# A hybrid layer on one core: the preparation of the scan shifted by a few empty steps, and the split values stored in full rows

## The chip, the core and the metric

The kernel runs on one core of a Trainium2 chip. The metric is the time that the device takes for one execution, in microseconds (us). A core has five engines that matter here, each with a queue of its own, worked in order: TensorE (PE in the profile, its weight loads PEld), VectorE (DVE), ScalarE (ACT), GpSimd (POOL) and SyncE (SP, which issues most DMA transfers). Matmul results go to PSUM banks, everything else lies in SBUF or in HBM.

## What is computed

One layer over 1024 latent tokens (with 256 context tokens ahead of them, 1280 rows in all) of width 1024. Its input projection has two groups of columns: a gated DeltaNet (4 heads of 128, scanned in both directions in chunks) and a neighbourhood attention (8 heads of 64). Both are concatenated and projected back; a SwiGLU feed-forward follows. The parts that matter here:

```
px = modulate(rms_norm(x, norm1_w[i]), sh1, sc1) @ w_in[i]       # q k v z a b | nq nk nv
qkv = short_conv(p[..., :3 * DN_WIDTH], conv_w)                    # centred, 5 taps, then SiLU
decay = exp(where(tril, gam[..., :, None] - gam[..., None, :], -inf))
m = where(strict, einsum("bhncd,bhnmd->bhncm", kb, k) * decay, 0)
u = triangular_solve(eye + m, v * beta[..., None])                 # and w, with the same matrix
...
s_win = einsum("bnqhd,binchd->bhnqic", q_r, k_r) + bias            # windows of 8 rows x 32 columns
o = einsum("bhnqic,binchd->bnqhd", p_win, v_r) + einsum("bhnqk,bkhd->bnqhd", p[..., n_win:], v_ctx)
...
x = x + g1 * (concatenate([dn_x, na_x], -1) @ w_out[i])
x = x + g2 * swiglu(modulate(rms_norm(x, norm2_w[i]), sh2, sc2), w_ffn_in[i], w_ffn_out[i])
```

The inverses of the triangular matrices `eye + m` (chunks of 128 rows here, 10 per direction) are needed by the scan.

## The kernel before

**Jobs.** The input projection is a list of jobs, worked one after the other (the loop in the code below). A `Block` makes 128 columns for all rows, transposed: 8 steps over the contraction, each with three matmuls (high and low halves of a value: high by high, low by high, high by low; `mm_part`, L404) for each of two or three column pieces. A `Wide` makes 256 columns with rows on the partitions, one tile of 128 rows after the other (L592), and each tile reads the whole of its weights `zw`. The order is k0 to k3, z (second half), nk0 to nk2, nv (first half), nk3, q0 to q3, nq0 to nq3, v0, nv (second half), v1, v2, v3, z (first half, called z0 in the prediction). Then come the scan and the attention, the output projection and the feed-forward.

**Weights.** A weight tile is loaded into `wraw`, of which there is one buffer. ScalarE casts its high part (`whi` L198, for a Wide `zw` L584), GpSimd computes the low part (`wlo` L199, `zw` L585). A Wide has two such halves, so its second load waits until GpSimd is done with the first. These loads stand in SyncE's queue.

**Behind a Block.** ScalarE copies its PSUM pieces into `cr` (L452), VectorE applies the five taps (L456, L460), ScalarE the SiLU (L467).

**Background work.** Two generators are advanced by a step at a time while the jobs run: one step for each of a Block's 8 steps, 2 or 3 for each tile of a Wide. A `yield` is the end of a step. The generators set where an instruction is traced; a scheduler then decides each engine's order, unless an instruction is pinned with `keep_in_program_order`, which puts it behind all that its engine was given earlier.

- `block_inverses` makes the inverses of the 32 by 32 diagonal blocks. VectorE works on `N` in a loop (L880, L882), the diagonal is set (L885), and after four empty steps TensorE transposes it in groups of four (L892) into PSUM banks `m`, which ScalarE copies out (L894). Results go to `x_d` in HBM.
- `preps` builds the full inverses, chunk by chunk in both directions, ten preparations in all, at most two of them alive at once. For a preparation GpSimd builds `rg` (L952), TensorE sums it into decays (L964, L965), ScalarE takes the exponential, VectorE scales the block `kk` (L971), TensorE multiplies by `fx` (L984), ScalarE copies the scaled block back into `kk` (L987), and three merges follow (TensorE L995, copies on VectorE L997 and on ScalarE L998), each in a step of its own. The results go to `y_d` and `at_d` in HBM (L1007). Between the sums and the products lie two steps, behind the copy one. Matmuls here use two banks called `pr`.

**The split values.** `nv` is stored to `nv_d` by rows. After each half, SyncE issues copies from there into `vw_d` (L1104), which holds the values by column block and row group as the windows of the attention need them. The attention reads them as `vw` (L277).

Of the kernel before, what the change touches and what calls it, by code (L numbers as in the profile page):

```python
# [88 lines left out]
def hybrid(ctx, tc, a, dbg):  # L89
# [56 lines left out]
    nv_d = dram.tile([T, 512], F32, name="nv_d", tag="nv_d")  # L146
    nq_d = dram.tile([NAH, 2, ND, L], F16, name="nq_d", tag="nq_d")
    nk_d = dram.tile([2, NAH, ND, T], F16, name="nk_d", tag="nk_d")
    vw_d = dram.tile([128, 4, 4, 4, 128], F32, name="vw_d", tag="vw_d")
    y_d = dram.tile([2, NCH, 128, 4, 128], F32, name="y_d", tag="y_d")  # L150
    at_d = dram.tile([2, 8, 128, 4, 128], F32, name="at_d", tag="at_d")
    x_d = dram.tile([128, 2, 2, NU, 32], F32, name="x_d", tag="x_d")
# [100 lines left out]
    def attention(nw):  # L253
# [20 lines left out]

        def values(hp, half, cb):
            vw = nw.tile([128, 3, 128], F32, name="vw", tag="vw", bufs=3)
            sp.dma_start(vw, vw_d[:, hp, cb, half:half + 3])  # L277
            return vw

        def context(hp):  # L280
# [93 lines left out]
    with ExitStack() as bs:  # L374
# [445 lines left out]
        def block_inverses():  # L820
            with ExitStack() as gs:
# [61 lines left out]
                    yield  # L883
                flat = N.rearrange("p b r c -> p b (r c)")
                dve.memset(flat[:P, :, 0:1024:33], 1.0)  # L885
                for _ in range(4):
                    yield
                U = WK.rearrange("p d u i -> p (d u) i")
                for i0 in range(0, 32, 4):
                    p = bank()  # L890
                    for i in range(4):
                        pe.transpose(p[:, i * P:(i + 1) * P], N[:P, :, :, i0 + i].rearrange("p b r -> p (b r)"),  # L892
                                     ident[:P, :P])
                    act.copy(U[:, :, i0:i0 + 4], p[:, :4 * P].rearrange("p (i u) -> p u i", i=4))  # L894
                    if i0 % 8 == 4:
                        yield
# [15 lines left out]
        def preps():  # L912

            first_half.close()
            with ExitStack() as gs:
                pk = pools(gs, "pk", "left")
                shift(gs, "ppad", "left", 64)
                pp = pools(gs, "pp", "left")

                def work(name, bufs=2, dt=F32):  # L920
                    return (pk if name == "kk" else pp).tile([128, 4, 128], dt, name=name, tag=name, bufs=bufs)

                fxs = [work(f"fx{d}", 1) for d in range(2)]
                ys = [[work(f"y{d}{i}", 1) for d in range(2)] for i in range(2)]
                for t in fxs + ys[0] + ys[1]:
                    pool.memset(t, 0.0)
                q32 = [slice(b * 32, b * 32 + 32) for b in range(4)]

                def fetch(i):

                    got = []
                    for d in range(2):
                        c = ORDER[d][i]
                        kk, xc = work("kk", 6), pp.tile([128, 2, 4, 32], F32, name="xc", tag="xc", bufs=4)
                        sp.dma_start(kk, kk_d[:, c])
                        sp.dma_start(xc, x_d[:, d, :, c * 4:c * 4 + 4])
                        at = None
                        if c >= 2:
                            at = work("at", 4)
                            sp.dma_start(at, qk_d[:, c - 2])  # L940
                        got.append((d, c, kk, xc, at))
                    return i, got

                def prep(i, got):
                    y = ys[i % 2]
                    rgs = []
                    for d, c, kk, xc, at in got:
                        mle = M[C_LE + d].rearrange("p (o i) -> p o i", o=1).to_broadcast([128, 4, 128])
                        for gg in (GH, GL):
                            rg = work("rg", 4, F32R)  # L950
                            g = gg.bitcast(F32)[:, d, c].rearrange("p (h o) -> p h o", o=1).to_broadcast([128, 4, 128])
                            pool.tensor_tensor(rg, g, mle, OP.mult)  # L952
                            rgs.append(rg)
                    for d, c, kk, xc, at in got:
                        for q in q32:
                            act.copy(fxs[d][q, :, q], xc[q, 1])
                    yield 1
                    if i == 0:
                        yield 1
                    es = []  # L960
                    for d, c, kk, xc, at in got:
                        p = bank("pr")
                        for j in range(2):
                            pe.matmul(p, mr[:, d], fl(rgs[2 * d + j]), start=j == 0, stop=False)  # L964
                        pe.matmul(p, mr[:, 4], mneg[:, d].rearrange("p (o i) -> p o i", o=1).to_broadcast(  # L965
                            [128, 4, 128]), start=False, stop=True)
                        e = work("e", 2)
                        act.activation(fl(e), p, AF.Exp)
                        es.append(e)
                    for (d, c, kk, xc, at), e in zip(got, es):  # L970
                        dve.tensor_tensor(kk, kk, e, OP.mult)  # L971
                    for (d, c, kk, xc, at), e in zip(got, es):
                        for q in q32:
                            pool.tensor_copy(y[d][q, :, q], xc[q, 0])
                        if at is not None:
                            dve.tensor_tensor(at, at, e, OP.mult)
                            stores.append((at_d[d, c - 2], at, tick[0] + 2))
                    yield 1
                    yield 1
                    ps = []  # L980
                    for d, c, kk, xc, at in got:
                        p = bank("pr")
                        for h in range(4):
                            pe.matmul(p[:, hs[h]], kk[:, h], fxs[d][:, h], start=True, stop=True)  # L984
                        ps.append(p)
                    for (d, c, kk, xc, at), p in zip(got, ps):
                        act.copy(fl(kk), p)  # L987
                    yield 1
                    for n in range(1, 4):
                        blk = (q32[3 - n], q32[n])  # L990
                        cols = (slice(128 - 32 * n, 128), slice(0, 32 * n))
                        ps = [bank("pr").rearrange("p (h i) -> p h i", h=4) for _ in got]
                        for h in range(4):
                            for (d, c, kk, xc, at), p in zip(got, ps):
                                pe.matmul(p[blk[d], h, :32 * n], kk[:, h, blk[d]], y[d][:, h, cols[d]],  # L995
                                          start=True, stop=True)
                        dve.tensor_copy(y[0][blk[0], :, cols[0]], ps[0][blk[0], :, :32 * n])  # L997
                        act.copy(y[1][blk[1], :, cols[1]], ps[1][blk[1], :, :32 * n])  # L998
                        yield 1
                    for d, c, kk, xc, at in got:  # L1000
                        stores.append((y_d[d, c], y[d], tick[0] + 1))

                stores, tick = [], [0]

                def flush(n):
                    while stores and stores[0][2] <= n:
                        sp.dma_start(*stores.pop(0)[:2])  # L1007

                todo = list(range(NCH))
                live, landing = [], []  # L1010
                while live or todo or landing:
                    if not landing and todo and (todo[0] < 2 or all(x in done for x in queries)):
                        landing.append(fetch(todo.pop(0)))
                    if landing and (not live or len(live) < 2 and live[0][1] >= 4):
                        live.append([prep(*landing.pop(0)), 0])
                    if not live:
                        yield
                    for g in list(live):
                        tick[0] += 1
                        flush(tick[0])  # L1020
                        g[1] += 1
                        if not next(g[0], 0):
                            live.remove(g)
                        yield
                flush(tick[0] + 2)
# [23 lines left out]
        for n in range(2, len(jobs) + 2):  # L1049
# [44 lines left out]
            for _ in fin:  # L1094
                pass
            done.add(n - 2)
            if isinstance(j, Wide) and j.kind == "nv":
                hv = slice(2 * j.half, 2 * j.half + 2)
                vlat = nv_d[CT:].rearrange("(r c) d -> r c d", c=64)
                for cb in range(4):  # L1100
                    for ch in range(4):
                        for r in range(4):
                            rows = vlat[4 * ch + r, BLKS[cb]:BLKS[cb] + 32].rearrange("c (h d) -> c h d", d=128)
                            sp.dma_start(vw_d[r * 32:r * 32 + 32, hv, cb, ch], rows[:, hv])  # L1104
            if nrm:
                nrm.norm()
            if isinstance(j, Block):
# [665 lines left out]
```

## Time and profile before

| | |
|---|---|
| median of 3 runs | 1541.6 us (1541.44 to 1543.45) |
| the profiled execution | 1541.49 us |
| its span on the core | 1539.4 us |
| mean granted clock of TensorE | 0.988 |
| busy: TensorE, VectorE, ScalarE, GpSimd | 1474.1, 993.6, 728.2, 234.8 us |
| `vw_d` stores: number, size, median landing | 128, 32.0 KB, 2.2 us |
| `vw` loads: number, size, median landing | 32, 192.0 KB, 3.8 us |

TensorE is busy for 96% of the span. What is left is a list of short waits, which the profile names by the waiting tile and line and by the instruction that ended the wait. The granted clock is the share of its full rate that TensorE was given. The edited stages lie between about 250 and 580 us of the span.

### The profile page before, as it was taken

To read this page: it belongs to the slowest core of one execution; us is meant where nothing else is said; L and a number is where in the kernel's file an instruction comes from. 1 tells how busy PE (TensorE), PEld (TensorE's weight loads), DVE (VectorE), ACT (ScalarE), POOL (GpSimd) and SP (SyncE) were. 2 spreads that over 40 slices of the span, in tenths; PEclk is the share of its full clock that TensorE was granted. 3 is DMA by queue.
4 is the path that set the end of the run, shared out by engine and by line. 5 is a ranking of instruction groups with operands and counts; after the bars stand their busy time and mean duration, and the time that the engine had idled before them with its cause. 6 is when DMAs were issued, how large, how long until landed. Compare 5 with 4: busy or idle time off the path is not lost. (4 is left out here: it accounts for less than half of the span.)

```text
span 1539.4 us, 24029 instructions
## 1 busy us (share of the span) xinstructions
PE 1474.1 (96%) x8702; PEld 1231.0 (80%) x8702; DVE 993.6 (65%) x1712; ACT 728.2 (47%) x1405; POOL 234.8 (15%) x286
## 2 busy tenths in 40 slices
PE   6999998899899898999999999999999999999999
PEld 3788797777688787788888878888888888888887
DVE  4774587974464354677977379855555566599652
ACT  5442552646764236666873176333333334354440
POOL 1054500634554100111210000000000000000000
PEclk9999999999999999999999999999999999999999
DMA  9274232687655557898638503533333334798742
GB/s 387 68 212 139 60 86 79 202 239 246 182 172 170 147 142 247 278 292 253 209 90 282 183 34 109 186 106 106 107 105 103 104 102 148 248 376 275 247 143 82
DMA packets 205142, 267.36 MB, mean 174 GB/s; under 512 B 17760, under 2 KB 115552, under 8 KB 204000
## 3 DMA queue, kind: packets, MB, share of 16 engines
q1 hardware_dynamic: 194320, 258.45, 52.4%
q10 hardware_dynamic: 10704, 7.38, 1.5%
q8 instruction: 68, 1.11, 0.3%
q14 instruction: 50, 0.41, 0.1%
HBM read 201.02 MB, written 68.94 MB: 175 GB/s over the span
## 5 line engine op out<-in xcount | busy, mean ns | idle before, releaser
L404 PE MATMUL blk<-hh,whi 128*128 128x512 f32 (+1 forms) x410 | 123.0, 394 | 6.8 <-ACT cr L452 5.3
L1410 ACT CAST uhi<-ws 128x512 fp32r<-128x512 f32 x91 | 54.0, 621 | 146.0 <-PE ps L1349 96.1
L1410 ACT CAST uhi<-wq 128x512 fp32r<-128x512 f32 x101 | 61.0, 622 | 130.9 <-issue 84.6
L404 PE MATMUL blk<-hl,whi 128*128 128x512 f32 (+1 forms) x410 | 115.4, 375 | 0.3 <-DVE hl L704 0.3
L404 PE MATMUL blk<-hh,wlo 128*128 128x512 f32 (+1 forms) x410 | 114.6, 375 | 0.6 <-POOL wlo L199 0.6
L592 PE MATMUL blk<-zw,hh 128*128 128x256 f32 (+1 forms) x576 | 113.5, 291 | 1.1 <-ACT cr L452 1.0
L1411 DVE TENSOR_TENSOR ulo<-wq,uhi 128x512 fp32r<-128x512 f32 x101 | 67.5, 687 | 58.4 <-ACT uhi L1410 32.4
L1349 PE MATMUL ps<-hT,uhi 128*128 128x512 f32 x336 | 103.6, 390 | 0.0
L1349 PE MATMUL ps<-lT,uhi 128*128 128x512 f32 x336 | 103.5, 389 | 0.0
L1349 PE MATMUL ps<-hT,ulo 128*128 128x512 f32 x336 | 103.4, 389 | 0.0
L592 PEld LDWEIGHTS blk<-zw,hh 128*128 128x128 f32 x576 | 91.7, 191 | 4.0 <-ACT cr L452 1.5
L1349 PE MATMUL ps<-hB,uhi 128*128 128x512 f32 x288 | 89.2, 391 | 0.6 <-ACT hB L1524 0.6
L1349 PE MATMUL ps<-lB,uhi 128*128 128x512 f32 x288 | 88.8, 389 | 0.4 <-DVE lB L1525 0.4
L1349 PE MATMUL ps<-hB,ulo 128*128 128x512 f32 x288 | 88.6, 389 | 0.0
L404 PEld LDWEIGHTS blk<-hh,whi 128*128 128x128 f32 x410 | 69.0, 194 | 21.9 <-ACT cr L452 6.1
L404 PEld LDWEIGHTS blk<-hl,whi 128*128 128x128 f32 x410 | 72.5, 192 | 14.9 <-DVE hl L704 0.8
L404 PEld LDWEIGHTS blk<-hh,wlo 128*128 128x128 f32 x410 | 72.5, 192 | 14.9 <-POOL wlo L199 0.9
L592 PE MATMUL blk<-zw,hl 128*128 128x256 f32 (+1 forms) x288 | 82.4, 286 | 0.0
L199 POOL TENSOR_TENSOR wlo<-wraw,whi 128x1024 fp32r<-128x1024 f32 x18 | 46.6, 2586 | 194.1 <-ACT whi L198 193.9
L1349 PEld LDWEIGHTS ps<-lT,uhi 128*128 128x128 f32 x336 | 63.1, 188 | 13.2
L1349 PEld LDWEIGHTS ps<-hT,ulo 128*128 128x128 f32 x336 | 63.1, 188 | 13.2
L1349 PEld LDWEIGHTS ps<-hT,uhi 128*128 128x128 f32 x336 | 62.9, 188 | 12.9
(362 smaller groups left out, 3526.1 us busy)
## 6 DMA issues: line engine op xcount, KB each, us to landing
wq<-w_fo SPq DMA_DIRECT2D x99, 256.0 KB, 4.1
wq<-w_gu SPq DMA_DIRECT2D x88, 256.0 KB, 2.9
wad<-wa SPq DMA_DIRECT2D x64, 256.0 KB, 4.2
bt<-rpb SPq DMA_DIRECT2D x64, 192.0 KB, 3.7
t_d<-g SPq DMA_DIRECT2D x22, 512.0 KB, 3.7
fr<-t_d SPq DMA_DIRECT2D x44, 256.0 KB, 5.2
f_d<-g SPq DMA_DIRECT2D x33, 256.0 KB, 2.1
fr<-f_d SPq DMA_DIRECT2D x33, 256.0 KB, 4.2
```

Source lines behind the costliest of these rows:

```text
L199: lo_engine.tensor_tensor(o, r, h.bitcast(F32), OP.subtract)
L404: pe.matmul(o, ww[:, k], xx[k][:, s], start=k == 0 and j == 0, stop=k == KT - 1 and j == 2)
L592: pe.matmul(p[:, :c1 - c0], x[k][:, s], ww[:, k, c0:c1], start=k == 0 and j == 0, stop=k == KT - 1 and j == 2)
L1349: pe.matmul(o, w[wi][:, k], x[xi][:, k], start=first and k == 0 and j == 0, stop=k == n - 1 and j == 2, skip_group_check=True)
L1410: act.copy(hi, self.raw[key])
L1411: dve.tensor_tensor(lo, self.raw[key], hi.bitcast(F32), OP.subtract)
```

## The change

Four edits. The transposes of the inverse come after six empty steps instead of four, and the first of each group is pinned to its place in program order. The first sums of preparation 0 come ten steps behind its `rg` instead of two (`LATE`; the ordinary step stays), and are pinned; the count that lets preparation 1 start begins lower by as much. Each preparation has one more empty step between the copy of the scaled block and the first merge. And `vw_d` holds full rows of 512 values: instead of 64 stores of 32 KB after each half of nv there are 16 stores of 256 KB after the second half, and a read of `vw` picks 128 of the 512 values in each of its three rows.

```
-    vw_d = dram.tile([128, 4, 4, 4, 128], F32, name="vw_d", tag="vw_d")
+    vw_d = dram.tile([128, 4, 4, 512], F32, name="vw_d", tag="vw_d")
...
-            sp.dma_start(vw, vw_d[:, hp, cb, half:half + 3])
+            sp.dma_start(vw, vw_d[:, cb, half:half + 3, hp * 128:hp * 128 + 128])
...
-                for _ in range(4):
+                for _ in range(6):
                     yield
...
-                        pe.transpose(p[:, i * P:(i + 1) * P], N[:P, :, :, i0 + i].rearrange("p b r -> p (b r)"),
-                                     ident[:P, :P])
+                        t = pe.transpose(p[:, i * P:(i + 1) * P], N[:P, :, :, i0 + i].rearrange("p b r -> p (b r)"),
+                                         ident[:P, :P])
+                        if not i:
+                            tc.keep_in_program_order(t)
...
                     yield 1
-                    if i == 0:
+                    for _ in range(LATE if i == 0 else 0):
                         yield 1
...
-                            pe.matmul(p, mr[:, d], fl(rgs[2 * d + j]), start=j == 0, stop=False)
+                            m = pe.matmul(p, mr[:, d], fl(rgs[2 * d + j]), start=j == 0, stop=False)
+                            if i == 0:
+                                tc.keep_in_program_order(m)
...
                         act.copy(fl(kk), p)
                     yield 1
+                    yield 1
...
-                stores, tick = [], [0]
+                LATE, stores, tick = 10, [], [0]
...
-                        live.append([prep(*landing.pop(0)), 0])
+                        live.append([prep(*landing.pop(0)), 0 if live or len(todo) < NCH - 1 else -LATE])
...
-            if isinstance(j, Wide) and j.kind == "nv":
-                hv = slice(2 * j.half, 2 * j.half + 2)
-                vlat = nv_d[CT:].rearrange("(r c) d -> r c d", c=64)
+            if isinstance(j, Wide) and n == values:
+                vlat = nv_d[CT:].rearrange("(n r c) d -> r c n d", r=4, c=64)
                 for cb in range(4):
-                    for ch in range(4):
-                        for r in range(4):
-                            rows = vlat[4 * ch + r, BLKS[cb]:BLKS[cb] + 32].rearrange("c (h d) -> c h d", d=128)
-                            sp.dma_start(vw_d[r * 32:r * 32 + 32, hv, cb, ch], rows[:, hv])
+                    for r in range(4):
+                        sp.dma_start(vw_d[r * 32:r * 32 + 32, cb], vlat[r, BLKS[cb]:BLKS[cb] + 32])
```

In the changed kernel the line numbers of `preps` are a little higher: the sums are L966 and L969, the products L988, the copy of the scaled block L991, the merges L1000 with their copies at L1002 and L1003, the stores L1012, the `vw_d` stores L1106.

**Where instructions move.** In the lists below a row is an engine's instruction in its order, `x8` is eight of them in a row; `hh` and `hl` are the high and low halves of the activations. First TensorE in the job q0, at the transposes of the inverse, before:

```order
L404 MATMUL blk<-hh_134,wlo 128x512 x2
L892 MATMUL m<-cst,N 128x80 x8
L404 MATMUL blk<-hh_451,whi 128x512 x2
L404 MATMUL blk<-hl_452,whi 128x512 x2
L404 MATMUL blk<-hh_451,wlo 128x512 x2
L892 MATMUL m<-cst,N 128x80 x8
```

And after:

```order
L404 MATMUL blk<-hh_134,wlo 128x512 x2
L404 MATMUL blk<-hh_451,whi 128x512 x2
L404 MATMUL blk<-hl_452,whi 128x512 x2
L404 MATMUL blk<-hh_451,wlo 128x512 x2
L404 MATMUL blk<-hh_453,whi 128x512 x2
L404 MATMUL blk<-hl_454,whi 128x512 x2
L404 MATMUL blk<-hh_453,wlo 128x512 x2
L892 MATMUL m<-cst,N 128x80 x8
```

The first group of transposes has moved behind twelve more matmuls, two steps of the Block; of the four groups the last now comes in the next job, behind the L491 matmuls that write the same banks.

Second, TensorE in a Block of nq, at preparation 3, from its products to its first merge (`pr<-y`), before:

```order
L984 MATMUL pr<-fx_2513,kk 128x128 x4
L984 MATMUL pr<-fx_2514,kk 128x128 x4
L404 MATMUL blk<-hh_130,whi 128x512 x2
L404 MATMUL blk<-hl_131,whi 128x512 x2
L404 MATMUL blk<-hh_130,wlo 128x512 x2
L995 MATMUL pr<-y_2517,kk 32x32
```

And after:

```order
L988 MATMUL pr<-fx_2461,kk 128x128 x4
L988 MATMUL pr<-fx_2462,kk 128x128 x4
L404 MATMUL blk<-hh_130,whi 128x512 x2
L404 MATMUL blk<-hl_131,whi 128x512 x2
L404 MATMUL blk<-hh_130,wlo 128x512 x2
L404 MATMUL blk<-hh_132,whi 128x512 x2
L404 MATMUL blk<-hl_133,whi 128x512 x2
L404 MATMUL blk<-hh_132,wlo 128x512 x2
L404 MATMUL blk<-hh_134,whi 128x512 x2
L404 MATMUL blk<-hl_135,whi 128x512 x2
L404 MATMUL blk<-hh_134,wlo 128x512 x2
L1000 MATMUL pr<-y_2465,kk 32x32
```

Eighteen matmuls stand now between the products and the merge that reads their copy, where six did. In the same way preparation 0 has moved: 36 matmuls more stand ahead of its first sums, and five rows of L404 between its products and its first merge.

Third, the end of v3. TensorE went from v3's last matmuls to the tiles of z0 before:

```order
L404 MATMUL blk<-hh_457,wlo 128x256
L404 MATMUL blk<-hh_457,wlo 128x512 x2
L592 MATMUL blk<-zw,hh_128 128x256
L592 MATMUL blk<-zw,hl_129 128x256
L592 MATMUL blk<-zw,hh_128 128x256
```

And after:

```order
L404 MATMUL blk<-hh_457,wlo 128x512 x2
L1000 MATMUL pr<-y_2465,kk 32x32 x4
L1000 MATMUL pr<-y_2466,kk 32x32 x4
L1000 MATMUL pr<-y_2465,kk 32x64 x4
L1000 MATMUL pr<-y_2466,kk 32x64 x4
L1000 MATMUL pr<-y_2465,kk 32x96
...
L1000 MATMUL pr<-y_2466,kk 32x96
L592 MATMUL blk<-zw,hh_128 128x256
```

The three merges of the last preparation now stand between v3 and z0; they were inside v1. ScalarE's queue in the same place (`cr` are the copies of a Block, `cacc` its SiLU, `zw` the two casts of z0's weights), before, from the copies of v1 on:

```order
L452 COPY cr<-blk 128x256
L452 COPY cr<-blk 128x512 x2
L584 COPY zw<-wraw 128x8x128
L467 ACT_TABLE_LOAD
L467 ACTIVATE cacc<-cacc 128x1280
L452 COPY cr<-blk 128x256
L452 COPY cr<-blk 128x512 x2
L467 ACTIVATE cacc<-cacc 128x1280
L584 COPY zw<-wraw 128x8x128
```

And after, from the SiLU of v2 on:

```order
L467 ACTIVATE cacc<-cacc 128x1280
L534 DMA v_d<-vt 128x10x128
L452 COPY cr<-blk 128x256
L452 COPY cr<-blk 128x512 x2
L1003 COPY y_2466<-pr 32x4x32
L1003 COPY y_2466<-pr 32x4x64
L467 ACTIVATE cacc<-cacc 128x1280
L1003 COPY y_2466<-pr 32x4x96
L584 COPY zw<-wraw 128x8x128 x2
```

The first cast stood ahead of v1's SiLU and of v2's copies, the second ahead of v3's copies; now both stand behind v3's SiLU and the copy of the last merge.

## The prediction

> **What bounds the kernel now.** I read the chain that ended last first, then TensorE's waits, then the granted clock by stretches, then the timeline around each wait that the change touches. The chain, on the page:
>
> ```profile
> PE ps L1349 27%; PE ps L1690 14%; DVE x L1531 0%; DVE lB L1525 0%; DVE ws L1406 0%; PE ps L218 0%; DVE x L1453 0%; DVE acc L1459 0%; PE ps L1443 0%; DVE xa L1697 0%; DVEq L1406 0%
> ```
>
> The end is TensorE multiplying without a pause. Nothing there is edited, so whatever TensorE loses or gains before it moves the end one for one. The edited stages run from 250 to 580 us, and TensorE waits there for these (us in total, times, longest):
>
> ```profile
> PE pr L995 <- ACT kk L987: 7.3, 6, 2.1
> PE m L892 <- DVE N L885: 5.7, 1, 5.7
> PE blk L404 <- ACT cr L452: 5.3, 1, 5.3
> ...
> PE pr L964 <- POOL rg L952: 2.7, 4, 0.9
> ...
> PE pr L984 <- DVE kk L971: 1.1, 1, 1.1
> ...
> PE blk L592 <- ACT cr L452: 1.0, 1, 1.0
> ```
>
> A wait also costs clock afterwards. In these stretches the third figure from the end (PEclk, ahead of DMA share and GB/s) is the granted clock:
>
> ```profile
> 250.00:260.00 10.00, 4.01 (x21) 3.00 (x20) 8.49 (x15) 0.41 (x1) 0.40 (x1) 0.79 0.19 52
> 260.00:265.00 5.00, 5.00 (x23) 4.05 (x23) 0.00 (x0) 1.30 (x4) 0.00 (x0) 0.73 0.43 125
> ...
> 290.00:300.00 10.00, 7.34 (x22) 4.85 (x21) 9.82 (x9) 3.76 (x7) 9.88 (x10) 0.67 0.77 235
> ...
> 395.00:405.00 10.00, 7.75 (x53) 5.57 (x53) 3.28 (x5) 7.72 (x17) 2.33 (x1) 0.83 0.41 106
> 440.00:450.00 10.00, 7.93 (x63) 7.39 (x62) 8.33 (x8) 7.75 (x18) 5.55 (x5) 0.83 0.49 133
> ...
> 530.00:535.00 5.00, 0.49 (x1) 0.49 (x2) 0.47 (x2) 4.40 (x6) 2.35 (x1) 0.73 1.07 248
> 535.00:540.00 5.00, 5.00 (x17) 4.10 (x17) 4.93 (x8) 0.44 (x1) 0.00 (x0) 0.59 1.09 277
> ```
>
> What a slow stretch loses is (1 − clock) × its length, less the part in which TensorE had nothing to do anyway. 395–405 and 440–450 lose 0.17 × 10 = 1.7 us each. 290–300 loses 3.3, of which I take 2.9 as worked time. 530–540 loses 1.35 + 2.05 = 3.4, less half of the 2.2 us still idle in it: 2.3. 250–265 loses 2.1 + 1.35 = 3.45, less half of some 2.4 us idle: 2.25.
>
> **The inverse's transposes, six empty steps for four.**
>
> ```profile
> 249.62 0.62 PE L404 MATMUL blk<-hh,whi 128*128 128x512 f32 x2
> ...
> 251.89 0.61 PE L404 MATMUL blk<-hh,wlo 128*128 128x512 f32 x2
> ...
> 257.96 0.38 DVE L882 TENSOR_TENSOR N<-N,tt 80x232 f32<-80x232 f32 x1
> 258.17 0.53 PE L892 MATMUL m<-cst,N 80*128 80x80 f32 x2 [5.66 <-DVE N L885]
> ```
>
> Ten matmuls start in 251.89 − 249.62 = 2.27 us, 0.228 us each. The first transposes now have 12 more of them ahead: 2.74 us of work in the place of as much waiting. VectorE's loop still ends when it did, so 2.92 of the 5.66 us stay: −2.7. The last of the four groups now lands behind the L491 matmuls, with which it shares two PSUM banks. Such a wait is not in the trace. It lies between 0 (the bank's copy was early) and 2.07 (the longest wait for a PSUM copy below); I take +1.2, nearer to the mean of those, 7.3 / 6. The clock after it: with 2.9 us idle one slow window of the two remains, and I count −0.55, between 0 and the −2.25 of the whole stretch.
>
> A rule to weigh here: the row at 397 us below shows a wait of 2.01 us and the 395–405 stretch at 0.83 right behind it. The Trainium skill, "TensorE: Matmul & The Clock Gate", Part 1, says that the clock is halved after a wholly idle window of about 3.4 us. By that rule a wait of 2.9 us would cost no clock and this term would be −2.25 instead of −0.55, 1.7 us faster; the row speaks against it, so I keep the smaller gain.
>
> **The first sums of preparation 0, ten steps for one.** The sums (L964) now come 36 matmuls later, 36 × 0.228 = 8.2 us.
>
> ```profile
> 290.52 1.20 POOL L952 TENSOR_TENSOR rg<-GH,cst 128x512 fp32r<-128x512 f32 x1
> ...
> 291.77 0.50 PE L964 MATMUL pr<-rg,mr 128*128 128x512 f32 x1 [0.94 <-POOL rg L952]
> ...
> 294.57 1.49 POOL L952 TENSOR_TENSOR rg<-GL,cst 128x512 fp32r<-128x512 f32 x1
> ```
>
> The last `rg` is ready at 296.06, and TensorE came to the first sums at 290.83 (0.94 us ahead of its L964 at 291.77). With 8.2 us of other work ahead it comes at 299, so the four waits of 2.7 us go, less 0.35 for the later start of GpSimd's chain behind the delayed transposes: −2.35 (bounds −2.7 and 0). The slow stretch that they cause goes too: −2.9. The wait for the scaled block (1.1) is halved, since the sums and what follows move together: −0.55.
>
> **The empty step behind the copy of the scaled block.** The six waits of 7.3 us come from merges that stand 6 to 9 matmuls behind the products which the copy reads:
>
> ```profile
> 391.89 1.95 PE L984 MATMUL pr<-fx,kk 128*128 128x128 f32 x16
> 397.24 0.25 PE L995 MATMUL pr<-y,kk 128*32 128x32 f32 x2 [2.01 <-ACT kk L987]
> ...
> 443.05 0.41 PE L995 MATMUL pr<-y,kk 128*32 128x32 f32 x8 [2.07 <-ACT kk L987]
> ```
>
> By the order they now stand 18 to 27 behind, 2.7 us or more of further work, and none waited longer than 2.07 at once. Only preparation 0 has five rows there; for it I leave 0.6. So −6.5 (with a 0.24 us second wait at 397 counted in), and the two slow stretches behind the waits of 2.01 and 2.07: −3.4. Bounds: 0 and −10.7. What is late next is preparation 9: it ends behind v3 rather than inside v1, which the next part prices.
>
> **The split values in full rows.** SyncE's queue, VectorE and ScalarE before:
>
> ```profile
> 490.92 30.98 SPq L1104 DMA_DIRECT2D vw_d<-nv_d  x46
> ...
> 525.45 0.61 SPq L583 DMA_DIRECT2D wraw<-w_z  x1
> ...
> 530.57 1.05 ACT L584 CAST zw<-wraw 128x1024 fp32r<-128x1024 f32 x1 [13.89 <-DMA wraw<-w_z]
> ...
> 534.51 0.80 PE L404 MATMUL blk<-hh,whi 128*128 128x512 f32 x1 [5.32 <-ACT cr L452]
> ```
>
> An issue takes 30.98 / 46 = 0.67 us. The load of the z weights stands behind them and lands 5.1 us after its issue; ScalarE's cast of it stands ahead of the copies of v2 (`cr`), and TensorE waits 5.32 us for those. Sixteen issues take some 11 us instead. The cast is also behind v3's copies now, so this wait goes whatever the load does: −5.3, and −2.3 of clock. The first burst (64 issues after the first nv half) held up no TensorE wait: nothing. The reads now take three pieces per partition; they are issued some 30 us ahead of their use: nothing, at worst one wait of a microsecond.
>
> **What it brings at the end of v3.** By the order, preparation 9's three merges stand behind all of v3 and directly ahead of z0's first tile; both casts of z0's weights stand on ScalarE behind SiLU of v3 and the last merge's copy. There is one raw buffer, so the second load waits for GpSimd's remainder of the first, and a z0 tile reads both halves. Before:
>
> ```profile
> 551.16 0.75 PE L404 MATMUL blk<-hh,wlo 128*128 128x256 f32 x3
> 552.94 0.38 PE L592 MATMUL blk<-zw,hh 128*128 128x256 f32 x1 [1.03 <-ACT cr L452]
> ...
> 553.92 5.90 DVE L460 SCALAR_TENSOR_TENSOR cacc<-cr,cw,cacc 128x255 f32<-128x255 f32 x6
> ...
> 559.86 1.28 ACT L467 ACTIVATE cacc<-cacc 128x1280 f32<-128x1280 f32 x1 [0.55 <-DVE cacc L460]
> ```
>
> ```profile
> L585 POOL TENSOR_TENSOR zw<-wraw,zw 128x1024 fp32r<-128x1024 f32 x6 | 14.8, 2462 | 25.9 <-ACT zw L584 25.9
> ...
> L584 ACT CAST zw<-wraw 128x1024 fp32r<-128x1024 f32 x6 | 6.3, 1046 | 26.2 <-DMA wraw<-w_z 13.9 <-DMA wraw<-w_nv 12.3
> ...
> L998 ACT COPY y<-pr 32x384 f32<-32x384 f32 x3 | 1.4, 473 | 6.7 <-DVE y L997 3.4 <-PE pr L995 3.3
> ...
> wraw<-w_nv SPq DMA_DIRECT2D x4, 512.0 KB, 4.3
> ```
>
> Count from T, the end of v3's matmuls (551.91 before). VectorE's convolution ended 559.82 − 551.91 = 7.9 us after it; two copies of the merges now stand among its operations, some 0.4 us each (ScalarE's largest takes 0.47): 8.7. SiLU 1.3: 10.0. Copy 0.47: 10.5. First cast 1.05: 11.5. First remainder 2.46: 14.0. Second load, 4.3 as the loads of 512 KB have it (5.1 for the one above): 18.3. Second cast: 19.4. Second remainder: 21.8, with the hand-overs some 22.1. Before, z0 began at T + 1.03. So +21.1, less 1.9 us of merges that now fill the wait: +19.2 (17 to 24). A wait that long halves the clock as the 5.32 us one did: +2.3. The attention's loads are issued behind the second z load, near T + 15, and are first read after four tiles of z0: nothing more.
>
> **The sum.** −2.7 + 1.2 − 0.55 (transposes), −2.35 − 2.9 − 0.55 (first sums), −6.5 − 3.4 (copies), −5.3 − 2.3 (the z cast at 530), +19.2 + 2.3 (z0) = −3.9 us. The profiled execution took 1541.49, the median of the runs is 1541.6: 1537.6, rounded to 1538.
>
> **Rivals.** First, slower: ScalarE's queue, not the merges' distance, sets the copies. At 397 the copy came late because ScalarE was busy with table loads and activations until then, and if the new order puts as much ahead of the copies again, the 9.9 us of that part stay: 1541.5 − 3.9 + 9.9 = 1547.5. It decides from about 7 us of them on. Against it: 12 more matmuls are 2.7 us, longer than any of the waits.
>
> Second, z0 is not held up: the casts run before v3's SiLU ends, or the merges are no longer ahead. Then only the gains stand: 1541.5 − 25.4 = 1516, and 1518 with the merges back on the path. Against it: ScalarE and TensorE take their instructions in order, and the first tile needs both halves.
>
> Third, the gains are smaller all round because slow stretches come back with new short waits (a bank, a late `rg`): each costs 1.7 to 2.9, and two bring the sum to zero or just above, 1541 to 1543.
>
> **How the numbers follow.** My sum, with its own range 1532 to 1544 (z0 −2 to +5, the bank wait 0 to 2, half a slow stretch either way), gets 0.56, more than half of it below 1538.5. The third rival lies inside that range's upper half and is counted there. The first rival gets 0.28 (1543 to 1552), the second 0.16 (1515 to 1525). The measurement can tell 0.2%, 3.1 us. Faster: 0.28 of my sum's 0.56 and the second rival, 0.44. Within: 0.20 of my sum and 0.04 of the first rival, 0.24. Slower: 0.08 and 0.24, 0.32. The range leaves out the second rival and the end of the first: 1527 to 1551.
>
> **What would show it.** In the changed kernel's waits the line of the merges (L1000) for `kk` should be under 1 us and that of L966 for `rg` gone; L892 should wait near 2.9. The granted clock should be full at 290–300, 395–405 and 440–450. SyncE should issue 16 `vw_d` stores. Ahead of z0's first L592 TensorE should stand idle for 15 us or more, released by GpSimd's L585, with ScalarE's L584 behind L467. A z0 that starts within 5 us of v3's end makes the prediction wrong on the fast side; waits above 7 us in total between 250 and 460 make it wrong on the slow side.

## The result, and the profile after

The changed kernel is slower: 1549.36 us in the median of four runs (1548.25 to 1552.7) beside 1541.52 us for the kernel before, a ratio of 1.0059 (95% interval 1.0044 to 1.0074). The span of the profiled execution grew from 1539.4 to 1546.5 us, by 7.1.

TensorE's waits in the changed kernel (us in total, times, longest), of those that answer to the ones shown before or took their place:

```profile
PE blk L592 <- ACT zw L584: 10.1, 1, 10.1
...
PE pr L1000 <- DVE y L1002: 7.9, 4, 5.1
...
PE pr L1000 <- ACT e L972: 3.3, 1, 3.3
...
PE m L485 <- ACT cr L470: 3.1, 1, 3.1
...
PE pr L1000 <- ACT kk L991: 2.1, 2, 1.4
```

The four waits for `rg` and the wait of v3 for v2's copies are gone from the list, and the waits for `kk` fell from 7.3 to 2.1 us. But merges now wait for the exponential and for copies of other merges, the row sums of q1 (L485) wait where they had not, and the wait of L592 for the casts of z0's weights (L584) and the longest of those for L1002 stand together at the end of v3. The timeline there:

```profile
535.82 0.75 PE L404 MATMUL blk<-hh,wlo 128*128 128x256 f32 x3
...
537.26 0.61 SPq L583 DMA_DIRECT2D wraw<-w_z  x1
...
542.21 1.49 PE L1000 MATMUL pr<-y,kk 128*32 128x64 f32 x16 [5.12 <-DVE y L1002]
...
545.33 1.27 ACT L467 ACTIVATE cacc<-cacc 128x1280 f32<-128x1280 f32 x1 [1.23 <-DVE cacc L460]
...
546.62 0.47 ACT L1003 COPY y<-pr 32x384 f32<-32x384 f32 x1
547.11 1.04 ACT L584 CAST zw<-wraw 128x1024 fp32r<-128x1024 f32 x1
548.29 2.34 POOL L585 TENSOR_TENSOR zw<-wraw,zw 128x1024 fp32r<-128x1024 f32 x1 [36.70 <-ACT zw L584]
550.66 0.60 SPq L583 DMA_DIRECT2D wraw<-w_z  x1
...
554.64 1.04 ACT L584 CAST zw<-wraw 128x1024 fp32r<-128x1024 f32 x1 [6.49 <-DMA wraw<-w_z]
...
555.74 0.58 PE L592 MATMUL blk<-zw,hh 128*128 128x256 f32 x1 [10.10 <-ACT zw L584]
...
558.17 0.79 PE L592 MATMUL blk<-zw,hh 128*128 128x256 f32 x2 [1.21 <-POOL zw L585]
```

v3 ends at 536.57, 15.3 us earlier than before (551.91). The convolution, the SiLU, the last merge's copy, the first cast, its remainder, the second load, the second cast and its remainder then follow one another as the prediction chained them, and z0's first full tile goes on at 558.17, 21.6 us after v3's end. Where TensorE stood, the clock fell, and it stayed low into z0 (PEclk is the third figure from the end):

```profile
540.00:555.00 15.00, 2.99 (x32) 2.40 (x32) 5.65 (x8) 3.50 (x5) 3.41 (x5) 0.50 0.33 110
555.00:565.00 10.00, 8.05 (x40) 7.76 (x41) 0.00 (x0) 1.06 (x2) 2.35 (x1) 0.55 1.08 268
```

For an account, take the start of the same matmul in both timelines (counted along L404, then along z0's):

| place | before | after | after − before |
|---|---|---|---|
| q0, ahead of the first edited TensorE instruction | 250.98 | 249.77 | −1.2 |
| behind the inverse's transposes | 275.65 | 271.35 | −4.3 |
| nq0, when preparations 0 and 1 are done | 357.69 | 352.36 | −5.3 |
| late in v2, when before has all ten done | 527.74 | 519.91 | −7.8 |
| end of v3 | 550.58 | 535.23 | −15.3 |
| in z0, its fifth tile | 566.10 | 573.41 | +7.3 |

From there to the end nothing more is gained or lost: the spans differ by 7.1 us.

These are single executions, and a row of 1 or 2 us in such a table is not safe. The kernel with half rows (below) was profiled twice, and the matmul of the first row started at 252.22 us in one and at 247.29 in the other. The run with z0's casts on GpSimd (below) has the same edits up to the end of v3; there the steps between the rows are −3.0, −1.1, −0.6 and −7.5, where the changed kernel has −3.1, −1.0, −2.5 and −7.5.

### The profile page after: what moved, and what is told of

Read it like the earlier page. It is cut to its first block, busy times and chain, and to the rows that moved or that the text cites. A ratio compares the mean times of both kernels' runs of the same rounds, so it can differ in the third digit from the quotient of the medians.

```text
span 1546.5 us, 23912 instructions
## 1 busy us (share of the span) xinstructions
PE 1471.3 (95%) x8702; PEld 1230.9 (80%) x8702; DVE 985.8 (64%) x1712; ACT 729.4 (47%) x1405; POOL 236.7 (15%) x286
## 5 line engine op out<-in xcount | busy, mean ns | idle before, releaser
L592 PE MATMUL blk<-zw,hh 128*128 128x256 f32 (+1 forms) x576 | 116.4, 295 | 12.5 <-ACT zw L584 10.1
L404 PE MATMUL blk<-hh,whi 128*128 128x512 f32 (+1 forms) x410 | 121.0, 389 | 1.4 <-ACT kk L549 1.4
L404 PE MATMUL blk<-hl,whi 128*128 128x512 f32 (+1 forms) x410 | 112.5, 371 | 0.3 <-DVE hl L704 0.3
L404 PE MATMUL blk<-hh,wlo 128*128 128x512 f32 (+1 forms) x410 | 111.8, 370 | 0.6 <-POOL wlo L199 0.6
L592 PEld LDWEIGHTS blk<-zw,hh 128*128 128x128 f32 x576 | 93.6, 194 | 16.1 <-ACT zw L584 10.4
L404 PEld LDWEIGHTS blk<-hh,wlo 128*128 128x128 f32 x410 | 71.3, 189 | 14.8 <-POOL wlo L199 0.9
L592 PE MATMUL blk<-zw,hl 128*128 128x256 f32 (+1 forms) x288 | 82.7, 287 | 0.0
L404 PEld LDWEIGHTS blk<-hl,whi 128*128 128x128 f32 x410 | 71.3, 189 | 14.3 <-DVE hl L704 0.8
L404 PEld LDWEIGHTS blk<-hh,whi 128*128 128x128 f32 x410 | 68.2, 191 | 16.3 <-issue 4.2
```

The lines of the kernel that those rows point to most:

```text
L404: pe.matmul(o, ww[:, k], xx[k][:, s], start=k == 0 and j == 0, stop=k == KT - 1 and j == 2)
L592: pe.matmul(p[:, :c1 - c0], x[k][:, s], ww[:, k, c0:c1], start=k == 0 and j == 0, stop=k == KT - 1 and j == 2)
```

## The experiments

Each run was timed beside the kernel before on the same chip, and the ratios are to that.

**Which edit makes z0 late?** First the changed kernel with the value stores of before:

```
-    vw_d = dram.tile([128, 4, 4, 512], F32, ...)       # 16 stores of full rows, once
+    vw_d = dram.tile([128, 4, 4, 4, 128], F32, ...)    # 64 stores after each half, as before
```

> The changed kernel with the value stores of before (128 of 32 KB, after each half of nv); the other three edits stay. Theory one: z0's late start (22 us between v3's end and z0's first full tile) comes from the rows edit, whose stores moved the two casts of z0's weights behind the SiLU of v3. Then z0 starts within 3 us of v3's end; but the casts stand ahead of v2's copies again, both of them now, and v3 waits for those copies for 8 to 11 us: 1536 to 1543 us. Theory two: the late start comes from the extra step, which moved preparation 9 to the end of v3. Then it stays: 1547 to 1551 us.

Ratio 1.0013 (0.9997 to 1.003), 1544.11 us. z0 starts on time, and v3 waits for v2's copies again:

```profile
PE blk L404 <- ACT cr L452: 2.2, 1, 2.2
```

So the late start hangs on the rows edit. That wait is 2.2 us and not the expected 8 to 11; a merge in v2 now waits 2.4 us ahead of it, and late in v2 TensorE is 4.5 us behind the kernel before. The time is one us above the expected 1536 to 1543. The profiled execution took 1540.38, so its waits do not explain that one us. Then the converse, the rows edit alone in the kernel before (the same lines, the other way round):

> The kernel before with the rows edit alone (16 value stores of 256 KB after the second half of nv). Theory one: the wait of 5.3 us in v3 goes with its slow clock (7.6 us), and z0 starts 18 to 21 us late with 2 to 4 us of clock: 1552 to 1558 us. Theory two: only the gain of 7.6 us shows: 1532 to 1536 us.

Ratio 1.0066 (1.0043 to 1.0089), 1551.64 us. The wait in v3 is gone, which brings the end of v3 from 551.91 to 543.55, and z0 begins at 561.87 after some of the attention's first products, 18.3 us behind v3's end. That is as theory one has it, 0.4 us under its range. One edit holds both the gain and the loss. And with the extra step taken out of the changed kernel:

```
                         act.copy(fl(kk), p)
                     yield 1
-                    yield 1
```

> The changed kernel without the extra step. Theory one: z0 starts as late as with it, and the copies' gain goes: 1549 to 1554 us. Theory two: the late start goes: 1527 to 1533 us.

Ratio 1.0041 (1.0025 to 1.0058), 1548.14 us: z0 is late without the extra step too, though the last merge there stands at 509.17 us, far ahead of v3's end. Theory two, that preparation 9 at the end of v3 is the cause, falls. The other half of theory one, that the copies' gain goes with the step, does not show: the time is one us under its range, and its ratio is no higher than the 1.0059 with the step.

**What is the extra step worth by itself?**

```
                         act.copy(fl(kk), p)
                     yield 1
+                    yield 1
```

> The kernel before with the extra empty step behind the copy of the scaled block alone. As predicted, the copies cost 9.9 us less between 300 and 460 us; as the changed kernel's trace has it, 2 to 4 us less, since merges then wait for other copies. Both casts of z0's weights stand ahead of v2's copies in its order, so v3 waits 3 to 6 us longer than before. By the prediction's size 1535 to 1538 us, by the trace's 1541 to 1546 us. If the extra step alone moved the end of v3 (theory two), 1555 us or more.

Ratio 1.0005 (0.999 to 1.0019), 1543.45 us: nothing that can be measured, where the prediction had put 9.9 us. In the kernel before, the waits for `kk` were 7.3 us; here these have come:

```profile
PE pr L984 <- ACT y L999: 5.1, 2, 3.6
...
PE pr L996 <- ACT e L968: 3.4, 1, 3.4
...
PE pr L984 <- DVE kk L971: 3.0, 1, 3.0
```

The zero hides one gain: v3's wait for v2's copies is 0.9 us there and not 5.3, as TensorE comes to it later. A pair of kernels in which v3 does not wait at all, with and without the step, follows below.

**Is it the order, or the stores?** The changed kernel with the same 16 stores, traced behind the loads and casts of z0's weights (which are themselves traced a little earlier, ahead of the attention; the scheduler still issued six of the stores ahead of the first load, from 484.7 to 504.1 us):

```
             if n == len(jobs) - 2:
                 ...
+                jobs[n + 1].prefetch()
+                vlat = nv_d[CT:].rearrange("(n r c) d -> r c n d", r=4, c=64)
+                for cb in range(4):
+                    for r in range(4):
+                        sp.dma_start(vw_d[r * 32:r * 32 + 32, cb], vlat[r, BLKS[cb]:BLKS[cb] + 32])
                 fill = attention(pools(attn, "nw", "left", 2))
```

> The changed kernel with the same 16 value stores traced later, behind the loads and casts of z0's weights (in v3's iteration, ahead of the attention). By the order both casts then stand ahead of v3's SiLU, the first even ahead of v2's copies, and preparation 9's merges lie inside v2 again. Theory one (it is the place of the casts, given by the order, that makes z0 late): z0 starts within 3 us of v3's end and the wait in v3 stays away, so the gain of 15 us at v3's end in the changed kernel's trace reaches the end of the program: 1525 to 1533 us. Theory three (the stores or their transfers themselves hold something up): 1538 us or more.

Ratio 0.9963 (0.9948 to 0.9978), 1535.21 us, faster than both kernels. The first load is issued at 511.50 instead of 537.26 and both casts are done before v3 ends:

```profile
511.50 0.61 SPq L583 DMA_DIRECT2D wraw<-w_z  x1
...
519.55 1.05 ACT L584 CAST zw<-wraw 128x1024 fp32r<-128x1024 f32 x1
...
527.89 1.07 ACT L584 CAST zw<-wraw 128x1024 fp32r<-128x1024 f32 x1
...
543.44 0.38 PE L592 MATMUL blk<-zw,hh 128*128 128x256 f32 x1 [1.03 <-ACT cr L452]
```

The stores are the same, so it is not their number and size that hold z0 up; their place in the order is. The time is 2 us above the expected range: v3 ends at 542.4 and not at 537, in part because 2.6 us of merges that stood behind v3 stand in v2 again, and of the lead of 9.5 us that the kernel has at v3's end 4.9 are left at the end of the program. The rest is lost between z0's later tiles and the attention's first products.

**Can the stores be few and still early?** In half rows, 16 of 128 KB after each half of nv:

```
+            if isinstance(j, Wide) and j.kind == "nv":
+                hv = slice(256 * j.half, 256 * j.half + 256)
...
+                        sp.dma_start(vw_d[r * 32:r * 32 + 32, cb, :, hv], vlat[r, BLKS[cb]:BLKS[cb] + 32, :, hv])
```

> The changed kernel with the stores in half rows, 16 of 128 KB after each half of nv. The order has the first cast of z0's weights ahead of v2's copies and the second right behind them. By theory one z0 starts on time; SyncE has half the queue of before in front of the weights' load, so v3 waits 0 to 4 us: 1526 to 1536 us. By theory three 1538 us or more.

Ratio 0.9941 (0.9921 to 0.9961), 1532.67 us: the wait in v3 is gone, and z0 follows v3's end as in the kernel before.

**The other two edits alone.** The later first sums in the kernel before (the lines with `LATE` and the pinned sums of the diff, nothing else):

> The kernel before with the later first sums of preparation 0 alone. The prediction's size: the four waits for rg and the slow stretch behind them go, 5.8 us, 1534 to 1537 us. By the changed kernel's trace the sums had stood ahead of the row sums of q1 (L485), which wait for ScalarE's squares (L470): that wait of 3 us and its slow stretch take their place, so only about 1 us is left: 1538 to 1542 us.

Ratio 1.0024 (1.0006 to 1.0042), 1545.25 us: no gain, and above both expected ranges (the runs spread from 1536.25 to 1550.46). The waits for `rg` have gone, and the wait for q1's squares has come:

```profile
PE m L485 <- ACT cr L470: 3.5, 1, 3.5
```

And the later transposes of the inverse alone:

> The kernel before with the inverse's later transposes alone. The prediction's size is 2.0 us, and the changed kernel's trace shows 3.1 us between 250 and 280 us: 1537 to 1540 us. If the work behind them (the stores of the inverse, preparation 0) starts later by as much, the gain is given back at the first sums: 1541 to 1543 us.

Ratio 1.0 (0.9984 to 1.0016), 1540.6 us, between the two ranges: no gain either. The wait fell to 2.9 us, and the waits for `kk` grew from 7.3 to 9.7. The four waits for `rg` went here too, without `LATE`, and the wait for q1's squares came in their place:

```profile
PE pr L997 <- ACT kk L989: 9.7, 6, 2.2
...
PE m L485 <- ACT cr L470: 3.1, 1, 3.1
...
PE m L892 <- DVE N L885: 2.9, 1, 2.9
```

In this order the first sums of preparation 0 stand at 301.52 us, behind q1's row sums at 296.14; in the kernel before they stood ahead of them. So either of the two edits alone takes the sums behind the row sums, and together they cannot gain that place twice.

**With z0 on time, what do the other edits bring?** Four kernels side by side. The half-row stores alone in the kernel before:

> The kernel before with the half-row value stores alone (16 of 128 KB after each half of nv; none of the other three edits). The order keeps the first cast of z0's weights ahead of v2's copies and the second ahead of v3's. If the shorter queue on SyncE is what the wait in v3 needed, that wait and its slow stretch go without a late z0: 7.6 us, 1532 to 1536 us. If another wait takes its place in v2 or v3: 1538 us or more.

Ratio 0.9941 (0.9922 to 0.996), 1533.25 us, as expected. The load of z0's weights is issued 8.5 us earlier than in the kernel before, and v3 no longer waits:

```profile
516.94 0.61 SPq L583 DMA_DIRECT2D wraw<-w_z  x1
```

The half rows with the other edits but without the extra step:

> The kernel with half-row stores and the other edits, but without the extra empty step. By the prediction's size of the copies, 9.9 us slower than with the step: 1540 to 1544 us. By the traces so far, which show 2 to 3 us of gain between 340 and 480 us: 1532 to 1538 us.

Ratio 0.993 (0.9913 to 0.9946), 1530.48 us, under both ranges. Without the later first sums:

> The kernel with half-row stores and the other edits, but without the later first sums of preparation 0. By the prediction's size 5.8 us slower than with them: 1537 to 1541 us. By the run of that edit alone, which gained nothing since the row sums of q1 waited instead: within 2 us of it, 1530 to 1536 us.

Ratio 0.9931 (0.9918 to 0.9945), 1530.37 us: within 2 us, as expected. And with all of them:

> The kernel with half-row stores and the other three edits once more, on the same chip as the three beside it: 1530 to 1535 us. It is what these are compared with, and shows whether 0.6% below the kernel before stands.

Ratio 0.9942 (0.992 to 0.9964), 1530.39 us. All four intervals overlap. The stores alone have the whole gain, as far as these intervals of 2 to 3 us to either side can tell; the extra step and the later sums bring nothing that they show, and 9.9 us for the step is far outside them. With the step, the waits are these:

```profile
PE pr L1000 <- ACT e L972: 3.3, 1, 3.3
...
PE pr L1000 <- DVE y L1002: 2.8, 3, 1.7
...
PE pr L966 <- ACT y L1003: 1.6, 1, 1.6
PE pr L988 <- ACT y L1003: 1.6, 1, 1.6
...
PE pr L1000 <- ACT y L1003: 1.2, 1, 1.2
...
PE pr L1000 <- ACT kk L991: 0.7, 1, 0.7
```

and without it these:

```profile
PE pr L999 <- ACT kk L991: 8.2, 7, 2.8
...
PE pr L988 <- DVE y L1001: 0.7, 2, 0.5
PE pr L999 <- POOL y L978: 0.7, 1, 0.7
```

8.2 us of waiting for `kk` became 0.7, and 10.5 us of waiting for the other users of the same two banks came (3.3 + 2.8 + 1.6 + 1.6 + 1.2), where there had been 1.4.

**What holds the merges now?** In the changed kernel the longest of the new waits ahead of v3's end, 3.3 us, ends when ScalarE gets past a cast that waits for its load:

```profile
404.49 1.04 ACT L584 CAST zw<-wraw 128x1024 fp32r<-128x1024 f32 x1 [5.54 <-DMA wraw<-w_nv]
405.56 1.09 ACT L972 ACTIVATE e<-pr 128x512 f32<-128x512 f32 x2
...
406.21 1.79 PE L1000 MATMUL pr<-y,kk 128*32 128x96 f32 x16 [3.33 <-ACT e L972]
```

So the half-row kernel was run with those casts on GpSimd:

```
-                    act.copy(self.hi[:, :, s], r)
+                    if self.kind == "nv" and self.half:
+                        pool.tensor_copy(self.hi[:, :, s], r)
+                    else:
+                        act.copy(self.hi[:, :, s], r)
```

> The kernel with half-row stores and the other three edits, and the casts of the second nv half on GpSimd instead of ScalarE. In the traces with the extra step the longest new wait among the preparations, 3.3 us at 402 us (a merge for a bank that the exponential holds), ends when ScalarE gets past such a cast, which waits 5.5 us for its load. If that is what took the copies' gain, the wait goes with its slow stretch: 3 to 5 us below the kernel with half-row stores, 1525 to 1529 us. If the two shared banks hold the merges in any case, or GpSimd's own queue is held instead, within 2 us of it: 1529 to 1533 us.

Ratio 0.9952 (0.9934 to 0.9971), 1531.36 us: no gain. The wait of 3.3 us is gone; the next one is longer, and it too ends behind a cast that waited for its load, this time v1's:

```profile
427.25 1.05 ACT L198 CAST whi<-wraw 128x1024 fp32r<-128x1024 f32 x1 [5.41 <-DMA wraw<-w_conv]
...
436.28 1.01 PE L991 MATMUL pr<-fx,kk 128*128 128x128 f32 x3 [5.79 <-ACT y L1006]
```

Between that cast and the copy for which TensorE waited (at 435.76) stand the copies of v0 and the activations of nq3 with their table loads, 7.5 us of ScalarE's own work. So that particular cast is not the cause. By the traces the next wait comes from ScalarE's queue again, at another place; no run gave the preparations a third bank or took their own copies off ScalarE, so whether the queue or the two banks set this limit is not shown.

**Is the casts' place the only reason for z0?** The changed kernel with z0's casts on GpSimd, which stood idle:

```
+                    if self.kind == "z" and not self.half:
+                        pool.tensor_copy(self.hi[:, :, s], r)
+                    else:
                         act.copy(self.hi[:, :, s], r)
```

> The changed kernel with both casts of z0's weights on GpSimd, which is idle there, instead of on ScalarE; ScalarE's order behind v3 no longer touches them. If it is the casts' place behind v3's SiLU that makes z0 late, z0 now starts within 6 us of v3's end: 1530 to 1537 us. If the first load of z0's weights is the floor (in the changed kernel's trace SyncE held it for 28.6 us, until a store of v that ScalarE issues at v3's end had landed), the load still comes at v3's end, and with 2.4 us for each cast on GpSimd z0 starts 17 to 21 us late as before: 1546 to 1551 us.

Ratio 1.0062 (1.0037 to 1.0086), 1549.87 us: z0 is as late as before, although the casts take 1.43 and 1.04 us on GpSimd and not 2.4. The load is a second floor under the first. SyncE's wait, and what followed:

```profile
SPq L583 <- DMA v_d<-vt: 28.6, 1, 28.6
```

```profile
532.60 0.38 ACTq L534 DMA_DIRECT2D v_d<-vt  x1
...
536.31 0.61 SPq L583 DMA_DIRECT2D wraw<-w_z  x1
...
540.35 1.43 POOL L585 CAST zw<-wraw 128x1024 fp32r<-128x1024 f32 x1 [29.71 <-DMA wraw<-w_z]
...
541.87 3.21 POOL L588 TENSOR_TENSOR zw<-wraw,zw 128x1024 fp32r<-128x1024 f32 x1
...
546.79 1.60 SPq L1015 DMA_DIRECT2D y_d<-y  x2
...
548.49 0.60 SPq L583 DMA_DIRECT2D wraw<-w_z  x1
```

z0 begins at 555.62, 20.0 us behind v3's end at 535.63. Not all of that is the first load's: the raw buffer was free at 545.08, and the second load was issued 3.4 us later, behind two stores of preparation 9 (`y_d`) that stand ahead of it in SyncE's queue and wait for the last merge's copies. Without them z0 would be some 16.6 us late, by these numbers an estimate.

The load has no data in common with the store of v that it waits for. In the trace the two report to the same semaphore, one of eight that SyncE's and ScalarE's transfers use in turn. The store landed at 536.25 and the load was issued at 536.31; in the changed kernel's own trace, with the same wait of 28.6 us, it is 537.19 and 537.26, and with the rows edit alone (a wait of 32.5 us) 544.18 and 544.24, on another of the eight. In the kernel before, no wait of SyncE at this line ends with a store of v. That the shared semaphore ties the two together is read off these times; no run gave the load one of its own. Nor did a run take this wait away and leave the casts where the changed kernel has them: that their place alone makes z0 late rests on the trace, in which the first load landed at 541.08 and its cast began at 547.11.

## Why the prediction was wrong

It forecast 1538 us, 1527 to 1551, and faster; the measured 1549.4 is inside that range, which had been stretched to take in most of the first rival, and on the other side of the kernel before. Step by step, with the differences of the table above:

| step | forecast | measured |
|---|---|---|
| transposes with their bank wait and clock | −2.05 | −3.1 (−4.3 + 1.2) |
| first sums, slow stretch, scaled block | −5.8 | −1.0 (−5.3 + 4.3) |
| copies of the scaled block, with clock | −9.9 | −0.6 (−7.8 + 5.3, less the prediction's 1.9 for the merges not yet done) |
| v3's wait for v2's copies, with clock | −7.6 | −7.5 |
| z0's late start, with clock | +21.5 | +20.8 (7.3 + 15.3, less the same 1.9) |

Ahead of the edits the profiled executions differ by 1.2 us of their own, and the stretches part the edits only roughly. The last two rows, the largest, were right to within 1 us, and the chain behind v3 was right link by link: 21.6 us from v3's end to the first full tile for a forecast of 22.1. One link was missing and did not matter: the first load came only at 537.26, held by the store of v, and the prediction had it waiting long since. It landed ahead of its cast all the same. The run with the casts on GpSimd shows that, without the forecast chain on ScalarE, it would still hold z0 up by some 17 to 20 us. That the missing link was the shorter of the two is luck.

**The step that failed is the copies,** "So −6.5 … and the two slow stretches behind the waits of 2.01 and 2.07: −3.4". The waits for `kk` did go, from 7.3 to 2.1 us, since 18 matmuls and more stand where six stood. What was not priced is what is late next, in that place; the prediction named preparation 9 at the end of v3 alone. Two preparations share two PSUM banks. By the traces, whoever keeps one of them behind its copy for a step longer puts its merges behind the other's sums, and then the merges wait for the exponential, and the products for the merges' copies. On ScalarE all of these stand in one queue with the casts and activations of the jobs. In the changed kernel the waits for these banks between 250 and 460 us add up to 10.0 us (3.3 + 2.1 + 1.6 + 1.1 + 0.8 + 0.6 + 0.5), beside 11.6 before (7.3 + 2.7 + 1.1 + 0.5), and the prediction had named 7 us as the sign that it was wrong on the slow side. The runs with and without the step, at 0.9942 and 0.993 of the kernel before, show no gain from it.

The time is that of the first rival (1547.5), which had 0.28, but the mechanism is only in part its own. It had the copies of the scaled block late again; here these were mostly in time, and other users of the same banks were late. That is nearer to the third rival, "new short waits (a bank, a late `rg`)", which was priced at two slow stretches, 1541 to 1543, and not at the whole gain.

**The second is the first sums,** −2.35 − 2.9 − 0.55. That "the four waits of 2.7 us go" was right. But the sums and the products were themselves what TensorE did while ScalarE finished q1's squares. Before, the row sums of q1 came at 311.74 and did not wait; after, TensorE is there at 293.84 and waits 3.1 us for a square that ends near 297, and the slow stretch that had followed the sums follows this wait:

```profile
290.00:300.00 10.00, 6.87 (x34) 5.86 (x33) 9.08 (x8) 5.46 (x10) 5.95 (x5) 0.89 0.60 201
300.00:305.00 5.00, 5.00 (x13) 3.90 (x14) 2.21 (x4) 1.97 (x3) 4.80 (x6) 0.55 0.98 322
```

The edit alone is no gain either (1.0024). The prediction named the cover of the moved sums and not what they had covered. It also added this gain to that of the transposes, although the later transposes alone already take the sums behind q1's row sums: with them, the half-row kernel takes the same time with and without `LATE`, within the intervals (0.9942 and 0.9931).

The transposes did better than forecast by 1 us: the bank wait taken at +1.2 came at 0.5 (L892 for ScalarE's L492, which reads the banks), and of the wait 2.06 us stayed and not 2.92. Alone, the edit is worth nothing in the end (1.0), as the row sums of q1 and the merges wait longer.

At the transposes the clock was weighed rightly. The wait of 2.06 us is followed by a stretch at 0.84, a loss of 1.6 us (0.16 × 10) where the prediction left 1.7:

```profile
256.07 0.45 PE L892 MATMUL m<-cst,N 80*128 80x80 f32 x2 [2.06 <-DVE N L885]
```

```profile
250.00:260.00 10.00, 7.53 (x31) 5.90 (x30) 6.46 (x13) 0.85 (x2) 0.00 (x0) 0.84 0.18 52
```

The Trainium skill, "TensorE: Matmul & The Clock Gate", Part 1, asks for an idle window of about 3.4 us before the clock is halved. The wait here is 2.06 us and the clock fell, so the measurement decides against it as a rule for single waits.

## What to carry to other kernels

When a wait of the bounding engine is to be removed, list what that engine reaches earlier by it, and what the work moved away had been covering: here the waits removed among the preparations, 3 to 7 us each, came back under other names, at the next user of the same two banks or of the same queue. When two edits move the same instructions, do not add their gains. A queue worked in order is as late as its first instruction that waits for a load, so look where a scheduler puts casts of freshly loaded weights, and with which other transfer a load shares a semaphore, when transfers ahead of them change in size. Cutting 128 small stores to 32 of 128 KB, issued as early as before, kept the casts in place and was worth 0.6% by itself; cutting them to 16 issued once moved the casts and cost as much.

## What the runs showed of the hardware that was not expected

A short wait is followed by slow clock or not, as it falls. The wait of L988 for a merge's copy is 1.60 us long in the changed kernel and in the run with the stores of before. In the changed kernel:

```profile
437.44 1.16 PE L988 MATMUL pr<-fx,kk 128*128 128x128 f32 x8 [1.60 <-ACT y L1003]
```

```profile
440.00:445.00 5.00, 3.87 (x39) 3.48 (x39) 4.94 (x7) 4.30 (x10) 2.17 (x3) 1.00 0.76 249
```

And with the stores of before:

```profile
439.54 1.62 PE L988 MATMUL pr<-fx,kk 128*128 128x128 f32 x8 [1.60 <-ACT y L1003]
```

```profile
440.00:445.00 5.00, 5.00 (x32) 5.00 (x31) 5.00 (x6) 2.85 (x7) 0.27 (x1) 0.66 0.90 290
```

Full clock behind the one, 0.66 behind the other: 1.7 us that a single profile has or has not (0.34 × 5).

After the long wait ahead of z0 more clock was lost than forecast. From z0's first matmul at 555.74 the stretch 555 to 565 has 0.55 of the clock on average, with TensorE busy for 8.05 of its 10 us; that cost some 3.6 us (8.05 × 0.45), where the prediction, from the wait of 5.3 us in v3, took 2.3.
